# One decoder block in fp32: a fixed engine order between mixer output and feed-forward, 128-column modulation products, and the root's bias in the last norm

## The chip, the cores and the metric

The kernel runs on one core of a Trainium2 chip. The metric is the device time of one execution in microseconds (us), as the median of several runs. Before the change it is 968.55 us (three runs, 968.13 to 969.51).

## The reference, cut to what matters

A decoder block over 512 tokens of width 1024: two parallel mixers (retention, short gated convolution), a sigmoid-gated merge, an output projection, and a SwiGLU feed-forward of width 2816. Both norms are modulated by vectors computed from a conditioning vector `c`. All data are float32.

```python
mod = silu(c) @ ada_w + ada_b
sh_m, sc_m, gt_m, sh_f, sc_f, gt_f = split(mod, 6)

h = rmsnorm(x, norm_mix_g) * (1 + sc_m) + sh_m
q, k, v, g_ret, b_cv, c_cv, u_cv, g_a, g_b = split(h @ w_in, ...)
y_a = (silu(g_ret) * y_ret) @ ret_w_out        # y_ret: retention of q, k, v
y_b = (b_cv * conv(c_cv * u_cv)) @ conv_w_out
merged = sigmoid(g_a) * y_a + sigmoid(g_b) * y_b
x = x + gt_m * (merged @ mix_w_out)

h = rmsnorm(x, norm_ffn_g) * (1 + sc_f) + sh_f
f = (silu(h @ ffn_w_gate) * (h @ ffn_w_up)) @ ffn_w_down
x = x + gt_f * f
return rmsnorm(x, final_norm_g)
```

## The kernel before, in words

**Products.** Every float32 operand is split into a high and a low part (`hi` is a cast on ScalarE, `lo` the difference on VectorE), and each product is three fast matmuls, low by high, high by low and high by high (`mm3`). Activations stand by feature, 128 features by 512 tokens, in `Hh`/`Hl` (input of the mixers) and `Gh`/`Gl` (input of the feed-forward). Weights come through three `raw` buffers of 1 MB each; a load waits until the split of an earlier weight has read its buffer. Four PSUM banks (`acc`) hold accumulators, two (`aux`) the transposes.

**Start.** In the first 20 us `x` is normalised and transposed. The modulation vectors of the first 256 features come from `ada_w`: TensorE takes three of the eight row blocks as products of `ada_m` with one column of `cs` (`mod_row`), VectorE sums the other five into `acc_m`, and `mod_sums` brings those sums to features by a product with one column of ones. These are plain float32 matmuls, so the trace shows two records for each. Products that nobody reads (`busy`, tile `idle`) stand between them. Then `mod_scale` and `mod_shift` make `a_m` and `s_m` on VectorE, ScalarE makes `Hh` from them, and the first projections (`p_c`, `p_u`, `p_b`, `p_k`) begin. The same happens for the feature blocks 2, 4 and 6, between halves of a block's 21 projection products. In this stage the order on each engine is written out: while an engine's `strict` flag is set, the wrapper `InTurn` (L62) ties each instruction behind the one before.

**Between mixers and feed-forward.** `tm_gemm` makes the output projection by token block: for each half `h` of the 1024 columns four groups `mix` of 128 tokens by 512, each of 24 matmuls. For `h == 1` `add_gated` forms the new `x1`, `half_ss` its sum of squares on ScalarE, and `norm2` the root, its reciprocal and the scaled rows `xn`; one group later eight transposes `tx`, the modulated `h`, `Gh` (ScalarE) and `Gl` (VectorE) follow. `first_ffn` computes the first 256 gate and up columns in two halves of 256 tokens (four accumulators by two halves by 24 matmuls), so that its first half needs token blocks 0 and 1 alone. The low parts of its up weights (`w_fu_l`) are made on GpSimd. No order is fixed here: a scheduler places the instructions.

**End.** The down projection's last part goes by token block. For each, `row_rstd` adds the two partial sums of squares on VectorE, takes the root on ScalarE with `eps_t` as its bias, and the reciprocal on VectorE; the two halves of the output leave by two transfers on SP's queue. The last token block is cut in two parts of 256 columns.

Of the kernel before, what the change touches and what calls it, by code (L numbers as in the profile page):

```python
# [70 lines left out]
def block_kernel(ctx, tc, x, c, positions, ada_w, ada_b, norm_mix_g, w_in, conv_w, ret_w_out,  # L71
# [179 lines left out]
    def row_rstd(s, name):  # L251
        r = sp.tile([P, 1], F32, tag="rr", name=name + "_r")
        vec.tensor_tensor(r, s[:, 0:1], s[:, 1:2], ALU.add)
        act.activation(r, r, AF.Sqrt, scale=1.0 / D, bias=eps_t)
        vec.reciprocal(r, r)
        return r

# [624 lines left out]
    def norm2(t):  # L882
        r = row_rstd(ss2[t], f"n2_{t}")
        xn = []
        for h in range(2):
            xn.append(scr(f"xn2_{t}{h}"))
            vec.tensor_scalar_mul(xn[h], x1[t][h], r)

        def rest():
            ts = slice(t * P, (t + 1) * P)  # L890
            for h in range(2):
                tx = aux(f"tx2_{t}{h}", [P, 4, P])
                for k in range(4):
                    nc.tensor.transpose(tx[:, k, :], xn[h][:, k * P:(k + 1) * P], ident)
                ks = slice(4 * h, 4 * h + 4)
                h32 = scr(f"h232_{t}{h}", F32, [P, 4, P])
                for k in range(4):
                    q = slice(4 * h + k, 4 * h + k + 1)
                    if k % 2:
                        act.activation(h32[:, k, :], tx[:, k, :], AF.Identity,  # L900
                                       scale=mod["a_f"][:, q], bias=mod["s_f"][:, q])
                    else:
                        vec.tensor_scalar(h32[:, k, :], tx[:, k, :], mod["a_f"][:, q],
                                          mod["s_f"][:, q], ALU.mult, ALU.add)
                act.copy(Gh[:, ks, ts], h32)
                vec.tensor_tensor(Gl[:, ks, ts], h32, Gh[:, ks, ts].bitcast(F32), ALU.subtract)

        after(1, rest)
# [13 lines left out]
    for h in range(2):  # L922
        groups = [acc(f"mix{h}_{t}") for t in range(NT)]
        for t in tm_gemm(mix_w_out[0], merged, 0, KT, h, groups, 4 if h == 0 else 0, "mix"):
            tick()
            add_gated(t, h, groups[t], "gt_m")
            half_ss(x1[t][h], ss2[t], h, f"n2_{t}")
            if h == 1:
                norm2(t)


    def first_ffn():

        ws, pts = list(early_w), [acc(f"p_fg0{i}") for i in range(2)]
        raw = load_raw(ffn_w_up[0], 0, KT, 0, 2 * P, "w_fu0")
        for i in range(2):
            ws.append(split(raw[:, :, i * P:(i + 1) * P], [P, KT, P], f"w_fu0{i}", pool))
            pts.append(acc(f"p_fu0{i}"))
        for half in range(2):
            for i in range(4):  # L940
                fm_gemm(pts[i], ws[i][0], ws[i][1], Gh, Gl, slice(half * HS, half * HS + HS))
                if half == 0 and i == 0:
                    tick()
                if half == 1 and i >= 2:
                    yield i - 2, pts[i - 2], pts[i]
# [96 lines left out]
```

## Time and profile before

| what | value |
|---|---|
| median of three runs | 968.55 us |
| time of the profiled execution | 968.18 us |
| its span, first to last instruction | 966.4 us |
| TensorE busy | 953.5 us, 99% of the span |
| VectorE, ScalarE, GpSimd busy | 556.9, 340.9, 14.9 us |
| mean granted TensorE clock | 0.995 |
| DMA | 120.98 MB, mean 125 GB/s |

The span leaves out 1.8 us of the execution's time. TensorE counts as busy while a matmul is in its pipeline, so 99% does not mean that matmuls follow each other as closely as they can. The granted clock is a share of 2.4 GHz: 0.5 is the lower level, 1.2 GHz.

### The profile page before, as it was taken

How to read it: one execution, taken by the hardware profiler on the slowest of the kernel's cores; microseconds unless marked ns; L12 is line 12 of the kernel's file. 1: busy time of each engine (PE TensorE's matmuls, PEld its weight loads, DVE VectorE, ACT ScalarE, POOL GpSimd, SP SyncE). 2: the span in 40 equal slices, each digit the busy share in tenths (PEclk: the TensorE clock that was granted, in tenths of full speed). 3: DMA queues.
4: the chain of work that ended last, by engine and by line, in shares of the span. 5: the costliest groups of instructions: out<-in, count | busy, mean ns of one | idle time of the engine just before them, and what ended most of it. 6: DMA issues, size and time to landing. Idle time of an engine off the chain costs nothing.

```text
span 966.4 us, 11389 instructions
## 1 busy us (share of the span) xinstructions
PE 953.5 (99%) x4647; PEld 807.1 (84%) x4647; DVE 556.9 (58%) x841; ACT 340.9 (35%) x505; POOL 14.9 (2%) x22
## 2 busy tenths in 40 slices
PE   8999999999999999999999998999999999999997
PEld 8898889888888888888888887988888888888886
DVE  5888875959674855654574458346533433333354
ACT  7534434444443423222223336423322122222223
POOL 2001000000000000000000002000000000000000
PEclk9999999999999999999999999999999999999999
DMA  9943233141222247774553542234433223331302
GB/s 307 335 150 119 89 98 98 55 142 55 87 87 88 86 122 189 213 190 138 174 178 125 175 131 63 91 126 150 161 98 121 87 87 89 119 120 66 110 1 87
DMA packets 109044, 120.98 MB, mean 125 GB/s; under 512 B 3700, under 2 KB 96928, under 8 KB 108992
## 3 DMA queue, kind: packets, MB, share of 16 engines
q1 hardware_dynamic: 108768, 120.08, 39.6%
q8 instruction: 36, 0.59, 0.3%
q0 software_dynamic: 224, 0.18, 0.1%
q14 instruction: 16, 0.13, 0.0%
HBM read 118.15 MB, written 2.10 MB: 124 GB/s over the span
## 4 chain that ended last, share of the span: by engine, by line
PE 94%; DVE 2%; DMA 1%; ACT 1%; issue 0%; SPq 0%; ACTq 0%; DVEq 0%
PE p_fu L64 12%; PE p_fg L64 12%; PE dn L64 12%; PE p_v L64 5%; PE p_ga L64 5%; PE p_gb L64 5%; PE p_yb L64 5%; PE p_ya L64 5%; PE mix L64 4%; PE p_q L64 4%; PE p_k L64 4%; PE p_g L64 3%; PE p_u L64 3%; PE p_b L64 3%; PE p_c L64 3%; PE y L64 2%
## 5 line engine op out<-in xcount | busy, mean ns | idle before, releaser
L64 PE MATMUL p_fu<-Gl,w_fu_h 128*128 128x512 f32 (+1 forms) x192 | 71.4, 372 | 0.0
L64 PE MATMUL p_fu<-Gh,w_fu_l 128*128 128x512 f32 (+1 forms) x192 | 71.3, 371 | 0.0
L64 PE MATMUL p_fu<-Gh,w_fu_h 128*128 128x512 f32 (+1 forms) x192 | 71.3, 371 | 0.0
L64 PE MATMUL dn<-w_dn_h,fa_l 128*128 128x512 f32 (+1 forms) x176 | 67.5, 384 | 0.0
L64 PE MATMUL dn<-w_dn_l,fa_h 128*128 128x512 f32 (+1 forms) x176 | 67.5, 383 | 0.0
L64 PE MATMUL dn<-w_dn_h,fa_h 128*128 128x512 f32 (+1 forms) x176 | 67.4, 383 | 0.0
L64 PE MATMUL p_fg<-Gh,w_fg_l 128*128 128x512 f32 x160 | 62.3, 389 | 0.0
L64 PE MATMUL p_fg<-Gl,w_fg_h 128*128 128x512 f32 x160 | 62.3, 389 | 0.0
L64 PE MATMUL p_fg<-Gh,w_fg_h 128*128 128x512 f32 x160 | 62.3, 389 | 0.0
L64 DVE TENSOR_TENSOR w_dn_l<-w_dn,w_dn_h 128x1024 fp32r<-128x1024 f32 x22 | 26.9, 1224 | 57.5 <-ACT w_dn_h L64 57.5
L64 DVE TENSOR_TENSOR w_fg_l<-w_fg,w_fg_h 128x1024 fp32r<-128x1024 f32 x20 | 24.5, 1224 | 56.0 <-ACT w_fg_h L64 56.0
L64 ACT CAST w_fu_h<-w_fu 128x1024 fp32r<-128x1024 f32 x22 | 23.2, 1053 | 71.3 <-PE p_fu L64 38.4
L64 ACT CAST w_dn_h<-w_dn 128x1024 fp32r<-128x1024 f32 x22 | 23.1, 1050 | 65.6 <-PE dn L64 39.5
L64 DVE TENSOR_TENSOR fg<-p_fu,fg 128x512 f32<-128x512 f32 x22 | 15.2, 690 | 49.2 <-PE p_fu L64 49.2
L64 PEld LDWEIGHTS p_fu<-Gh,w_fu_h 128*128 128x128 f32 x192 | 36.2, 188 | 6.2
L64 PEld LDWEIGHTS p_fu<-Gl,w_fu_h 128*128 128x128 f32 x192 | 36.2, 188 | 6.2
L64 PEld LDWEIGHTS p_fu<-Gh,w_fu_l 128*128 128x128 f32 x192 | 36.2, 188 | 6.2
L64 ACT ACTIVATE fg<-p_fg 128x512 f32<-128x512 f32 x22 | 13.2, 598 | 79.6 <-PE p_fg L64 79.6
L64 PEld LDWEIGHTS dn<-w_dn_h,fa_l 128*128 128x128 f32 x176 | 33.1, 188 | 6.7
L64 PEld LDWEIGHTS dn<-w_dn_l,fa_h 128*128 128x128 f32 x176 | 33.1, 188 | 6.5
L64 PEld LDWEIGHTS dn<-w_dn_h,fa_h 128*128 128x128 f32 x176 | 33.1, 188 | 6.4
L64 PE MATMUL p_v<-w_v_h,Hh 128*128 128x256 f32 x128 | 36.2, 283 | 0.0
(343 smaller groups left out, 2522.0 us busy)
## 6 DMA issues: line engine op xcount, KB each, us to landing
w_fg<-in_ffn_w_gate_dram SPq DMA_DIRECT2D x11, 1024.0 KB, 5.4
w_fu<-in_ffn_w_up_dram SPq DMA_DIRECT2D x11, 1024.0 KB, 5.5
w_dn<-in_ffn_w_down_dram SPq DMA_DIRECT2D x10, 1024.0 KB, 5.0
ada_m<-in_ada_w_dram SPq DMA_DIRECT2D x32, 256.0 KB, 6.1
ada_f<-in_ada_w_dram SPq DMA_DIRECT2D x32, 256.0 KB, 4.3
...
```

Source lines behind the costliest of these rows:

```text
L64: self.last = op(*args, **kw)
```

## The change

It has four parts.

1. **Modulation products.** `mod_row` and `mod_sums` stream 128 equal columns (a broadcast of `cs`, all of `ones32`) where they streamed one, and the vectors are read from every 128th column. At the start all four products of row block 7 stand ahead of the sums, and two `busy` products follow instead of four.
2. **Mixer output to feed-forward.** For `h == 1` the order on TensorE, VectorE and ScalarE is written out. The transposes of a token block stand three matmuls before the end of the next group. VectorE's second `Gl` and ScalarE's second `Gh` of a block go behind the scaled rows of the next one.
3. **No GpSimd there.** The low parts of the first up weights are made on VectorE (`up_lo`), one ahead of token block 2's modulation, one ahead of token block 3's. In `first_ffn` the second up column block runs once over 512 tokens instead of twice over 256.
4. **Last norm.** The sum over the first half of the columns is scaled and increased by `EPS` as soon as it is there, and the root takes it as its bias, so that the addition on VectorE ahead of the root goes. The very last transfer is issued from ScalarE's queue.

The core of the diff:

```diff
         for i in cols:
-            mm(banks[i % 2][:, i:i + 1], lhsT=ada_raw["m", j][k][:, i * P:(i + 1) * P],
-               rhs=cs[:, k:k + 1], start=first and (i == 0 or i == 1 and banks is apart), stop=False)
+            mm(banks[i % 2][:, i * P:(i + 1) * P], lhsT=ada_raw["m", j][k][:, i * P:(i + 1) * P],
+               rhs=cs[:, k:k + 1].to_broadcast([P, P]),
+               start=first and (i == 0 or i == 1 and banks is apart), stop=False)
...
-            mm(banks[i % 2][:, i:i + 1], lhsT=a[:, i * P:(i + 1) * P], rhs=ones32[:, 0:1],
+            mm(banks[i % 2][:, i * P:(i + 1) * P], lhsT=a[:, i * P:(i + 1) * P], rhs=ones32,
...
-    mod_row(0, 7, apart, False, (0, 1, 2))
+    mod_row(0, 7, apart, False)
     mod_sums(a, apart, False, (0, 2))
-    mod_row(0, 7, apart, False, (3,))
     mod_sums(a, apart, False, (1, 3))
-    busy(4)
+    busy(2)
...
+    def mixed(t, k):
+        if t == 3 and k == 3:
+            up_hi(0)
+            up_lo(0)
+        if t and k == 6:
+            norm2_transposed(t - 1)
+            norm2_mod(t - 1, 0, vec)
+            for h in range(2):
+                norm2_mod(t - 1, h, act)
+            norm2_hi(t - 1, 0)
+
+    groups = [acc(f"mix1_{t}") for t in range(NT)]
+    for t in tm_gemm(mix_w_out[0], merged, 0, KT, 1, groups, 0, "mix", between=mixed):
+        pe.strict = vec.strict = act.strict = True
+        add_gated(t, 1, groups[t], "gt_m")
+        half_ss(x1[t][1], ss2[t], 1, f"n2_{t}")
+        if t:
+            norm2_mod(t - 1, 1, vec)
+        norm2_scaled(t)
+        if t:
+            norm2_hi(t - 1, 1)
+            norm2_lo(t - 1, 1)
...
+        part(0, 0, KT, halves[0])
+        part(1, 0, 5, halves[0])
+        up_hi(1)
+        up_lo(1)
+        norm2_transposed(3)
+        for h in range(2):
+            norm2_mod(3, h, vec)
+            norm2_mod(3, h, act)
+            norm2_hi(3, h)
+            norm2_lo(3, h)
+        pe.strict = vec.strict = act.strict = False
+        part(1, 5, KT, halves[0])
+        part(2, 0, KT, halves[0])
+        part(0, 0, KT, halves[1])
+        part(2, 0, KT, halves[1])
+        yield 0, pts[0], pts[2]
+        part(1, 0, KT, halves[1])
+        part(3, 0, KT, slice(0, S))
+        yield 1, pts[1], pts[3]
...
+                        vec.tensor_scalar(ss3[t][:, 0:1], ss3[t][:, 0:1], 1.0 / D, EPS, ALU.mult,
+                                          ALU.add)
...
-                r = row_rstd(ss3[t][:, cs.start // HS:], f"nf_{t}")
+                r = sp.tile([P, 1], F32, tag="rr", name=f"nf_{t}_r")
+                i = 1 + cs.start // HS
+                act.activation(r, ss3[t][:, i:i + 1], AF.Sqrt, scale=1.0 / D, bias=ss3[t][:, 0:1])
+                vec.reciprocal(r, r)
...
-                    nc.sync.dma_start(o2[t, i], o)
+                    (nc.sync if i or t < NT - 1 else nc.scalar).dma_start(o2[t, i], o)
```

The instructions move at three places. The first is TensorE's queue ahead of the first projection. `mods` and `p_k_126` are the two banks that take the modulation products, `acc_m_262` is VectorE's sum. Before:

```order
L62 MATMUL idle<-ident 128x128 x5
L62 MATMUL mods<-cs,ada_m_4_141 128x1
L62 MATMUL p_k_126<-cs,ada_m_4_141 128x1
L62 MATMUL mods<-cs,ada_m_4_141 128x1
L62 MATMUL mods<-ones_84,acc_m_262 128x1 x2
L62 MATMUL p_k_126<-cs,ada_m_4_141 128x1
L62 MATMUL p_k_126<-ones_84,acc_m_262 128x1 x2
L62 MATMUL idle<-ident 128x128 x4
L62 MATMUL p_c_290<-Hh,w_c_0_h 128x512
```

And now:

```order
L62 MATMUL idle<-ident 128x128 x5
L62 MATMUL mods<-cs,ada_m_4_141 128x128
L62 MATMUL p_k_126<-cs,ada_m_4_141 128x128
L62 MATMUL mods<-cs,ada_m_4_141 128x128
L62 MATMUL p_k_126<-cs,ada_m_4_141 128x128
L62 MATMUL mods<-ones_84,acc_m_262 128x128 x2
L62 MATMUL p_k_126<-ones_84,acc_m_262 128x128 x2
L62 MATMUL idle<-ident 128x128 x2
L62 MATMUL p_c_288<-Hh,w_c_0_h 128x512
```

The fourth product of row block 7 moved ahead of the sums, all have 128 columns, and two idle products are gone.

The second place is VectorE's queue from token block 1's modulation to token block 2's scaled rows. `h_1x` and `h_2x` are the modulated blocks, `n_2_r` is token block 2's root, `xn_2x` its scaled rows. Before:

```order
L64 TENSOR_SCALAR h_10_4875<-tx_10_4870,a_f,s_f 128x128
L64 TENSOR_SCALAR h_11_4887<-tx_11_4882,a_f,s_f 128x128
L64 TENSOR_TENSOR x_2_1_4549<-x_2_1_4549,dx_gt_m_0_4894 128x512
L64 TENSOR_TENSOR Gl<-h_10_4875,Gh 128x4x128
L64 TENSOR_TENSOR Gl<-h_11_4887,Gh 128x4x128
L64 TENSOR_TENSOR n_2_r<-n2s_4564 128x1
L64 RECIPROCAL n_2_r<-n_2_r 128x1
L64 TENSOR_SCALAR xn_20_4903<-x_2_0_4548,n_2_r 128x512
L64 TENSOR_SCALAR xn_21_4905<-x_2_1_4549,n_2_r 128x512
L64 TENSOR_TENSOR w_fg_l<-w_fg_5216,w_fg_h 128x1024
L64 TENSOR_SCALAR h_20_4936<-tx_20_4931,a_f,s_f 128x128
```

And now:

```order
L62 TENSOR_TENSOR x_2_1_4547<-x_2_1_4547,dx_gt_m_0_4887 128x512
L62 TENSOR_SCALAR h_11_4880<-tx_11_4870,a_f,s_f 128x128 x2
L62 TENSOR_TENSOR n_2_r<-n2s_4562 128x1
L62 TENSOR_TENSOR Gl<-h_10_4875,Gh 128x4x128
L62 RECIPROCAL n_2_r<-n_2_r 128x1
L62 TENSOR_SCALAR xn_20_4899<-x_2_0_4546,n_2_r 128x512
L62 TENSOR_SCALAR xn_21_4901<-x_2_1_4547,n_2_r 128x512
L62 TENSOR_TENSOR Gl<-h_11_4880,Gh 128x4x128
L62 TENSOR_TENSOR w_fu_lo<-w_fu_4917,w_fu_hi 128x1024
L62 TENSOR_SCALAR h_20_4942<-tx_20_4932,a_f,s_f 128x128 x2
```

One `Gl` now stands between the root's sum and its reciprocal, the other behind the scaled rows, and the first up weight's low part ahead of the next modulation.

The third place is the same queue at token block 3, the last one. Before:

```order
L64 TENSOR_SCALAR xn_30_4964<-x_3_0_4550,n_3_r 128x512
L64 TENSOR_SCALAR xn_31_4966<-x_3_1_4551,n_3_r 128x512
L64 TENSOR_SCALAR h_30_5015<-tx_30_5010,a_f,s_f 128x128
L64 TENSOR_SCALAR h_31_5027<-tx_31_5022,a_f,s_f 128x128
L64 TENSOR_SCALAR h_30_5015<-tx_30_5010,a_f,s_f 128x128
L64 TENSOR_SCALAR h_31_5027<-tx_31_5022,a_f,s_f 128x128
L64 TENSOR_TENSOR Gl<-h_30_5015,Gh 128x4x128
L64 TENSOR_TENSOR Gl<-h_31_5027,Gh 128x4x128
L64 TENSOR_TENSOR fg_0_5178<-p_fu_4980,fg_0_5178 128x512
```

And now:

```order
L62 TENSOR_SCALAR xn_30_4966<-x_3_0_4548,n_3_r 128x512
L62 TENSOR_SCALAR xn_31_4968<-x_3_1_4549,n_3_r 128x512
L62 TENSOR_TENSOR Gl<-h_21_4947,Gh 128x4x128
L62 TENSOR_TENSOR w_fu_lo<-w_fu_4917,w_fu_hi 128x1024
L62 TENSOR_SCALAR h_30_5033<-tx_30_5023,a_f,s_f 128x128 x2
L64 TENSOR_TENSOR w_fg_l<-w_fg_5190,w_fg_h 128x1024 x2
L62 TENSOR_TENSOR Gl<-h_30_5033,Gh 128x4x128
L62 TENSOR_SCALAR h_31_5040<-tx_31_5028,a_f,s_f 128x128 x2
L62 TENSOR_TENSOR Gl<-h_31_5040,Gh 128x4x128
L64 TENSOR_TENSOR fg_0_5128<-p_fu_4978,fg_0_5128 128x512
```

Three subtractions of whole weight blocks (`w_fu_lo`, `w_fg_l` twice) now stand between token block 3's scaled rows and its `Gl`.

## Rows read from the trace of the kernel before

**Rows 1.** The page: busy shares, and the chain that ended last by engine.
```profile
PE 953.5 (99%) x4647; PEld 807.1 (84%) x4647; DVE 556.9 (58%) x841; ACT 340.9 (35%) x505; POOL 14.9 (2%) x22
...
PE 94%; DVE 2%; DMA 1%; ACT 1%; issue 0%; SPq 0%; ACTq 0%; DVEq 0%
```
**Rows 2.** Stretches: us, busy us of each engine (instructions), PEclk, DMA share, GB/s.
```profile
18.00:20.00 2.00, 2.00 (x12) 2.00 (x12) 1.35 (x6) 1.67 (x3) 0.00 (x0) 0.54 1.11 342
20.00:22.00 2.00, 2.00 (x9) 1.72 (x9) 1.76 (x4) 1.97 (x5) 0.00 (x0) 0.61 1.09 346
...
595.60:597.60 2.00, 1.99 (x10) 1.99 (x11) 1.80 (x3) 1.28 (x3) 0.00 (x0) 0.50 0.85 257
```
**Rows 3.** Timeline of PE, start: start us, us, what, [idle before <-releaser].
```profile
2.10 5.11 PE L62 MATMUL idle<-ident 128*128 128x128 f32 x34
...
14.79 1.36 PE L62 MATMUL idle<-ident 128*128 128x128 f32 x10
...
17.12 0.78 PE L62 MATMUL mods<-ones,acc_m 128*128 128x1 f32 x4 [0.30 <-DVE acc_m L62]
...
18.70 2.06 PE L62 MATMUL idle<-ident 128*128 128x128 f32 x8
20.41 1.20 PE L62 MATMUL p_c<-Hh,w_c_h 128*128 128x512 f32 x2
...
24.25 0.62 PE L62 MATMUL p_c<-Hl,w_c_h 128*128 128x512 f32 x2
```
**Rows 4.** Timeline of VectorE and ScalarE, start.
```profile
17.94 0.22 DVE L62 SCALAR_TENSOR_TENSOR a_m<-mods,vecs,b_m 128x1 f32<-128x1 f32 x1 [0.48 <-PE mods L62]
...
18.33 0.81 ACT L62 ACTIVATE Hh<-xT,s_m,a_m 128x512 fp32r<-128x512 f32 x1 [0.54 <-DVE s_m L62]
...
21.55 0.69 DVE L62 TENSOR_TENSOR Hl<-xT,Hh 128x512 fp32r<-128x512 f32 x1
```
**Rows 5.** Timeline of PE at feature block 4.
```profile
40.38 0.95 PE L62 MATMUL mods<-ones,acc_m 128*128 128x1 f32 x8
41.19 0.71 PE L62 MATMUL p_c<-Hl,w_c_h 128*128 128x512 f32 x2
```
**Rows 6.** Timeline of GpSimd, 540 to 620 us.
```profile
588.71 2.41 POOL L64 TENSOR_TENSOR w_fu_l<-w_fu,w_fu_h 128x1024 fp32r<-128x1024 f32 x1 [494.25 <-ACT w_fu_h L64]
592.00 2.48 POOL L64 TENSOR_TENSOR w_fu_l<-w_fu,w_fu_h 128x1024 fp32r<-128x1024 f32 x1 [0.89 <-ACT w_fu_h L64]
```
**Rows 7.** Timeline of VectorE, 565 to 612 us.
```profile
580.14 0.68 DVE L64 TENSOR_TENSOR dx_gt_m<-mix,gt_m 128x512 f32<-128x512 f32 x1
...
584.45 0.88 DVE L64 TENSOR_SCALAR xn<-x,n_r 128x512 f32<-128x512 f32 x2
...
589.87 2.40 DVE L64 TENSOR_TENSOR Gl<-h,Gh 128x512 fp32r<-128x512 f32 x2 [1.44 <-ACT Gh L64]
592.19 2.31 DVE L64 TENSOR_TENSOR n_r<-n2s 128x1 f32<-128x1 f32 x1
```
**Rows 8.** Timeline of PE, 555 to 625 us.
```profile
585.08 1.06 PE L894 MATMUL tx<-ident,xn 128*128 128x128 f32 x8
...
592.90 0.28 PE L64 MATMUL p_fg<-Gl,w_fg_0h 128*128 128x256 f32 x1
595.61 1.97 PE L894 MATMUL tx<-ident,xn 128*128 128x128 f32 x8 [2.43 <-DVE xn L64]
```
**Rows 9.** The chain that ended last: start us, us, what.
```profile
614.81 5.76 PE p_fu L64 x48
620.57 10.91 PE p_fg L64 x48
```
**Rows 10.** Timeline of VectorE, ScalarE and SP's queue, end.
```profile
961.46 0.16 DVE L64 TENSOR_TENSOR nf_r<-nfs 128x1 f32<-128x1 f32 x1 [0.18 <-ACT nf_j L64]
...
961.66 0.29 ACT L64 ACTIVATE nf_r<-nf_r,eps_t 128x1 f32<-128x1 f32 x1 [0.23 <-DVE nf_r L64]
...
963.12 0.38 SPq L1006 DMA_DIRECT2D out_dram<-o  x1
```

More of the change, by code (lines that the diff above doesn't have):

```diff
@@ L249, in half_ss @@
         act.activation(junk[:, 0:part.shape[-1]], part, AF.Square, accum_out=s[:, h:h + 1])
[L251 to L256, printed above, removed]
     ang, angh, ah = misc("ang"), misc("angh", F32R), misc("ah")
@@ L476, in block_kernel @@
     for k in range(2):
-        mod_scale("m", k, apart[k][:, 2 + k:3 + k])
-        mod_shift("m", k, apart[k][:, k:k + 1], 1)
+        mod_scale("m", k, apart[k][:, (2 + k) * P:(2 + k) * P + 1])
+        mod_shift("m", k, apart[k][:, k * P:k * P + 1], 1)
     w_hi("c", 0)
@@ L514, in block_kernel @@
         w_lo("c", j)
-        mod_cols("m", j, mods)
+        mod_cols("m", j, mods.rearrange("p (i n) -> p i n", n=P)[:, :, 0])
         for k in (j, j + 1):
@@ L833, in block_kernel, with tm_gemm @@
             gate_vec("gt_m")
-    def tm_gemm(src, acts, k0, nk, h, groups, early, name, cut=False):
+    def tm_gemm(src, acts, k0, nk, h, groups, early, name, cut=False, between=None):
         ws = []
@@ L864, in tm_gemm @@
                 one(k, i)
+                if between:
+                    between(part[0], k)
             yield part if cut else part[0]
@@ L880, in block_kernel @@
     ss2 = [sp.tile([P, 2], F32, tag="ss", name=f"n2s_{t}") for t in range(NT)]
-    def norm2(t):
-        r = row_rstd(ss2[t], f"n2_{t}")
-        xn = []
-        for h in range(2):
[L886 to L908, printed above, removed]
@@ new lines, in block_kernel, with norm2_scaled, norm2_transposed @@
+    xn2, h2, tx2 = {}, {}, {}
+    def norm2_scaled(t):
+        r = sp.tile([P, 1], F32, tag="rr", name=f"n2_{t}_r")
+        vec.tensor_tensor(r, ss2[t][:, 0:1], ss2[t][:, 1:2], ALU.add)
+        act.activation(r, r, AF.Sqrt, scale=1.0 / D, bias=eps_t)
+        if t:
+            norm2_lo(t - 1, 0)
+        vec.reciprocal(r, r)
+        for h in range(2):
+            xn2[t, h] = scr(f"xn2_{t}{h}")
+            vec.tensor_scalar_mul(xn2[t, h], x1[t][h], r)
+    def norm2_transposed(t):
+        for h in range(2):
+            tx2[t, h] = aux(f"tx2_{t}{h}", [P, 4, P])
+            for k in range(4):
+                transpose(tx2[t, h][:, k, :], xn2[t, h][:, k * P:(k + 1) * P], ident)
@@ new lines, in norm2_mod @@
+    def norm2_mod(t, h, eng):
+        if (t, h) not in h2:
+            h2[t, h] = scr(f"h232_{t}{h}", F32, [P, 4, P])
+        for k in range(4):
+            q = slice(4 * h + k, 4 * h + k + 1)
+            if k % 2 and eng is act:
+                act.activation(h2[t, h][:, k, :], tx2[t, h][:, k, :], AF.Identity,
+                               scale=mod["a_f"][:, q], bias=mod["s_f"][:, q])
+            elif not k % 2 and eng is vec:
+                vec.tensor_scalar(h2[t, h][:, k, :], tx2[t, h][:, k, :], mod["a_f"][:, q],
+                                  mod["s_f"][:, q], ALU.mult, ALU.add)
@@ L910, in block_kernel, with norm2_hi, norm2_lo @@
+    def norm2_hi(t, h):
+        act.copy(Gh[:, 4 * h:4 * h + 4, t * P:(t + 1) * P], h2[t, h])
+    def norm2_lo(t, h):
+        g = slice(4 * h, 4 * h + 4), slice(t * P, (t + 1) * P)
+        vec.tensor_tensor(Gl[:, g[0], g[1]], h2[t, h], Gh[:, g[0], g[1]].bitcast(F32),
+                          ALU.subtract)
     early_w = []
@@ L920, in block_kernel @@
         early_w.append((wh, wl))
[L922 to L929, printed above, removed]
-    def first_ffn():
[L934 to L945, printed above, removed]
+    groups = [acc(f"mix0_{t}") for t in range(NT)]
@@ new lines, in block_kernel, with up_hi, up_lo @@
+    for t in tm_gemm(mix_w_out[0], merged, 0, KT, 0, groups, 4, "mix"):
+        tick()
+        add_gated(t, 0, groups[t], "gt_m")
+        half_ss(x1[t][0], ss2[t], 0, f"n2_{t}")
+    wu = []
+    def up_hi(i):
+        if i == 0:
+            wu.append(load_raw(ffn_w_up[0], 0, KT, 0, 2 * P, "w_fu0"))
+        hi, lo = (wp.tile([P, KT, P], F32R, tag=z, name=f"w_fu0{i}_{z}") for z in ("hi", "lo"))
+        act.copy(hi, wu[0][:, :, i * P:(i + 1) * P])
+        wu.append((hi, lo))
+    def up_lo(i):
+        hi, lo = wu[1 + i]
+        vec.tensor_tensor(lo, wu[0][:, :, i * P:(i + 1) * P], hi.bitcast(F32), ALU.subtract)
@@ new lines, in first_ffn, with part @@
+    def first_ffn():
+        pts = [acc(f"p_f{m}0{i}") for m in "gu" for i in range(2)]
+        def part(i, k0, k1, ts):
+            for k in range(k0, k1):
+                wh, wl = (w[k] if isinstance(w, list) else w[:, k, :] for w in (early_w + wu[1:])[i])
+                mm3(pts[i][:, ts], wh, wl, Gh[:, k, ts], Gl[:, k, ts], k == 0, k == KT - 1)
+        halves = [slice(i * HS, (i + 1) * HS) for i in range(2)]
+        part(0, 0, KT, halves[0])
[3 more added lines that the diff above has]
+        norm2_transposed(3)
+        for h in range(2):
+            norm2_mod(3, h, vec)
[11 more added lines that the diff above has]
+        yield 1, pts[1], pts[3]
@@ L993, in block_kernel @@
                     xg[t] = scr(f"xg_{t}")
-                else:
-                    vec.tensor_tensor(ss3[t][:, 1:2], ss3[t][:, 0:1], ss3[t][:, 1:2], ALU.add)
+                if cs.stop < S:
+                    vec.scalar_tensor_tensor(ss3[t][:, 0:1], ss3[t][:, 1:2], 1.0 / D,
+                                             ss3[t][:, 0:1], ALU.mult, ALU.add)
                 vec.tensor_tensor(xg[t][:, cs], x1[t][h][:, cs], fg[h][:, cs], ALU.mult)
```

2 lines of the change are left out of this document (added).

## The prediction

> **What bounds the kernel now.** I read the page first: TensorE is busy for 99% of the span and makes 94% of the chain that ended last [rows 1]. So a change pays only where TensorE waits, runs at its lower clock, or has finished while others still work. The table of stretches then shows where the clock is low: the granted clock is 0.54 and 0.61 from 18 to 22 us and 0.50 from 595.6 to 597.6 us, which is the 1.2 GHz level [rows 2]; everywhere else it is close to 1.00. TensorE's timeline shows the waits around these two places, and the timeline's last microseconds the third place, where TensorE has ended. The change touches exactly these three, so I price each alone.
>
> **Start, part 1 of the change.** Before the clock falls, TensorE has run one-column products with two waits between them [rows 3]. The four idle products at 18.70 then take 1.71 us until the first `p_c` at 20.41; at the pace of the idle products at 14.79 (ten records to the next row, 0.12 us each) they would take 0.96. `Hh`, which `p_c` needs, was ready at 19.14 (18.33 plus 0.81) [rows 4]. So `p_c` starts 1.27 us later than its data allow. It then runs at half clock for another microsecond: its 15th matmul stands at 24.25, 3.84 us after the first, where 14 at 0.227 us (10.91/48 [rows 9]) are 3.18. In the changed order, two idle products fewer let TensorE be free at about 18.45, before `Hh`. The sums end a little sooner too, since their wait ended at 17.12 and at full clock two of them need 0.24 each and then their latency, so I put `a_m` 0.1 to 0.2 us earlier than 17.94 and `p_c` at about 19.05. If the clock stays at 2.4 GHz the 15th matmul then stands at 22.3: **1.95 us** earlier. Next in line behind it is `Hl`, ready at 22.24 before [rows 4] and some 0.15 us sooner now, which just fits.
>
> The clock is the assumption here. The nearest row for it is the start itself: idle products of 128 columns and transposes fill most of the time up to 14 us, and the granted clock stays at 1.00 until the one-column products prevail. I take it that the changed products look like the idle ones.
>
> Against this stands what 128 columns cost. On TensorE's path lie the four products and four sums of feature block 2 and the four sums each of blocks 4 and 6: 16 products, 32 records. One column takes 0.101 us a record (41.19 less 40.38, by 8 [rows 5]). For 128 columns the lowest row is the idle one at 14.79, 0.12 us a record; the highest is the first idle stretch, 5.11 us by 34, 0.15 us [rows 3]. By these two rows the cost is 0.6 to 1.6 us; a gain is excluded, since no product goes away. Eight transposes of 128 columns fit into 1.06 us with the last one's latency [rows 8], which suggests that even 0.12 is high, so I take **0.4 us** and keep 1.6 for the range.
>
> The Trainium skill (TensorE: Matmul & The Clock Gate, section Back-to-back issue gap) speaks against these columns: a warm matmul of up to 64 columns takes about 60 cycles, one of 128 takes 134. As an estimate from that page the 32 records cost 1.0 us more, and the sum below would be 5.7 instead of 6.3. The trace does not agree for this kernel, since a one-column record already takes 0.101 us [rows 5], four times those 60 cycles.
>
> Start: 1.95 less 0.4 is 1.55 us.
>
> **Mixers to feed-forward, parts 2 and 3.** TensorE stops between the `p_fg` matmul at 592.90 and the transposes at 595.61: 2.71 us, of which 0.12 is the matmul's own pace (5.76/48 [rows 9]). It waits for `xn` on VectorE [rows 8]. VectorE's rows say why: two `Gl` subtractions take 2.40 us together, where 0.69 is normal for one of this size [rows 4], and an addition of 128x1 takes 2.31, where 0.16 is normal [rows 10]. They end within a tenth or two of GpSimd's two subtractions (588.71 to 591.12, 592.00 to 594.48) [rows 6, 7]. So VectorE stands while GpSimd's instruction runs, once for over 1 us and once for 2.1. The transposes then take 1.97 us instead of 1.06 [rows 8], and the clock is low [rows 2] until about 598.3. From 595.6 to 598.3 TensorE does the work of 1.35 us, so 1.35 is lost. With GpSimd gone both losses go: 2.6 plus 1.35.
>
> What comes in its place? VectorE gets two subtractions of 128x1024, some 1.2 us each (a little under twice the 0.69 of one half as wide [rows 4]), at places where it must be on time. Before, the chain from a group's end to its scaled rows took 5.2 us (580.14 to 585.33) [rows 7]. In the new order TensorE has 21 matmuls until it needs them, 4.8 us. The new order takes one `Gl` (0.6 us of VectorE) and one `Gh` cast out of this chain and puts them behind it, and lets the other `Gl` run while ScalarE takes the root; that leaves 4.2 us by the same rows, half a microsecond of room. For token block 3 the room is 3 `mix` and 40 `p_fg` matmuls of 0.12 with no transposes between, 5.5 us, less 0.7 for the group's own last three; the chain is again some 4.2 plus 0.6 that VectorE is late because of `w_fu_lo`. This is about even. Last, the second half of `first_ffn` needs token block 3's `Gl`: VectorE reaches it after `w_fu_lo` and two `w_fg_l`, 3.6 us, from about 597, and ends it near 602.4; TensorE asks at about 602.35 (23 of 24 `p_fu` matmuls behind the transposes). Even again; I put no stall there, and up to one in the range.
>
> The second up column block runs 24 matmuls of 512 columns (0.227 us) instead of 48 of 256 (0.12): 5.76 less 5.45 is 0.3 us saved [rows 9]. The three matmuls that now follow the transposes move no work. The raw buffer of the first up weights is released about 4 us later than GpSimd released it, which delays a load that is used 30 us later: nothing.
>
> Transition: 2.6, 1.35 and 0.3 are **4.25 us**.
>
> **End, part 4.** From the addition `nf_r` at 961.46 to the root at 961.66 is 0.20 us [rows 10]. It goes once for token block 2, behind which VectorE's last stretch is queued without a gap, and once for token block 3: 0.4 us, less 0.05 for the longer fused sum. The last transfer is issued at 963.12 on SP's queue, right behind another; an issue takes 0.38 us there [rows 10]. On ScalarE's queue it need not wait for that one. No row shows an issue from ScalarE. Bounds are 0.4 us better (the other issue's time) and 0.2 worse (an issue half as long again). I take 0.15. The four small VectorE instructions for the bias stand where VectorE waits for matmuls. End: **0.5 us**.
>
> **Sum.** 1.55, 4.25 and 0.5 are 6.3 us off the profiled execution's 968.18: 961.9 us. The three runs' median is 0.4 above that execution; I don't add it, as two of the three runs and the profile lie within 0.4 us.
>
> **The rivals.**
>
> *The clock falls at the start all the same.* For it: two waits remain (for `acc_m` and for `Hh`), and the transposes and waits around them are the same. Against: the rows before 14 us. Then `p_c` starts at 19.05 at half clock and 2.35 us until 21.4 do half the work: 1.2 us less gain, 963.1 us.
>
> *Columns paid in full.* At 0.15 us a record, 1.6 us instead of 0.4: 963.1 us. The skill's figures above would make it 962.5.
>
> *A wait at token block 3.* The two `w_fg_l` and `w_fu_lo` stand ahead of `Gl` on VectorE. It decides as soon as VectorE is late at `h_30`; then TensorE waits up to the two `w_fg_l`, 2.3 us: 964.2 us.
>
> *GpSimd is not what holds VectorE.* If the stretched rows come from something else (a transfer, ScalarE), the wait stays: only 2.05 and 0.3 are gained, 965.9 us. Against it: both stretched rows end with GpSimd's.
>
> *Slower: the fixed order waits three times.* In the free order a late `xn` lets TensorE go on with other matmuls; now each of three transposes stands ahead of matmuls that don't need it. If the chain from a group's end to `xn` took 7.5 us instead of 4.2, each place would stop TensorE as long as the one before did, with the low clock behind it: three times 3.95 us, 11.85, on top of 961.9, which makes 973.7. It loses against before from about 2.1 us per place on. Against it: the longest such chain without GpSimd is 5.2 us.
>
> **How the numbers follow.** The forecast has 0.63, the clock 0.12, the columns 0.08, the wait at token block 3 0.10, GpSimd not guilty 0.05, the three waits 0.02. A measurement of this kernel tells about 0.2%, 1.9 us, from no change. Below 966.6 lie all but the last case, with some room for what I have not seen: faster 0.95, within 0.2% 0.03, slower 0.02. The range takes in the first four cases with a microsecond of small errors in the terms: 960.3 to 964.6.
>
> **What would show it.** Right: granted clock near 1.00 from 18 to 22 us and the first `p_c` near 19; no wait of TensorE over 0.5 us from 573 to 620 and a VectorE addition `n_r` of 0.16 us; a chain without `nf_r` on VectorE ahead of the root. Wrong: a clock near 0.5 in either place, `tx` rows that wait for `xn`, `p_fg` or `p_fu` rows that wait for `Gl`, or a last transfer that lands later after ScalarE's last instruction than before.

## The result and the profile after

The changed kernel takes **961.90 us** (median of four runs, 961.56 to 962.06) against 968.34 us for the kernel before (its three runs and a fourth of 966.57): a ratio of 0.9935 with a 95% interval of 0.9917 to 0.9952. Forecast were 961.9 us and a gain of over 0.2%; both came. The profiled execution took 962.06 us, its span is 960.3 us. One later execution of the kernel before took 1603.95 us at a granted clock of 0.555 and is left out of every number here.

The page's busy shares and chain, which answer to [rows 1]:

```profile
PE 949.9 (99%) x4619; PEld 802.7 (84%) x4619; DVE 555.9 (58%) x843; ACT 340.1 (35%) x505; POOL 10.1 (1%) x20
...
PE 96%; DVE 2%; ACT 1%; DMA 1%; issue 0%; SPq 0%; ACTq 0%
```

Busy TensorE time fell by 3.6 us with only 28 records fewer, so over half of the 6.1 us that went was time in which TensorE counted as busy. GpSimd lost two instructions of 2.4 us.

Stretches of the changed kernel (columns as in [rows 2]), the start and the passage to the feed-forward:

```profile
18.00:20.00 2.00, 1.60 (x12) 1.37 (x12) 1.17 (x5) 1.35 (x3) 0.00 (x0) 1.00 1.08 339
20.00:22.00 2.00, 2.00 (x11) 1.62 (x10) 1.76 (x4) 2.00 (x4) 0.00 (x0) 1.00 1.10 348
...
594.00:598.00 4.00, 4.00 (x36) 4.00 (x36) 3.91 (x9) 3.68 (x6) 0.00 (x0) 1.00 0.00 0
```

The granted clock is 1.00 where it was 0.54, 0.61 and 0.50. TensorE's timeline of the changed kernel, against [rows 3, 8]:

```profile
18.51 0.61 PE L62 MATMUL idle<-ident 128*128 128x128 f32 x4
19.51 0.73 PE L62 MATMUL p_c<-Hh,w_c_h 128*128 128x512 f32 x2 [0.40 <-ACT Hh L62]
...
22.82 0.62 PE L62 MATMUL p_c<-Hl,w_c_h 128*128 128x512 f32 x2
...
595.74 1.04 PE L62 MATMUL tx<-ident,xn 128*128 128x128 f32 x8
```

The first `p_c` now waits for its data (`Hh`), not for idle products, and the transposes of token block 3 wait for nothing. VectorE's timelines of the changed kernel, at the start against [rows 4] and in the passage against [rows 7]:

```profile
18.26 0.22 DVE L62 SCALAR_TENSOR_TENSOR a_m<-mods,vecs,b_m 128x1 f32<-128x1 f32 x1 [0.58 <-PE mods L62]
```

```profile
587.16 0.16 DVE L62 TENSOR_TENSOR n_r<-n2s 128x1 f32<-128x1 f32 x1 [0.31 <-ACT n_j L62]
587.24 0.68 DVE L62 TENSOR_TENSOR Gl<-h,Gh 128x512 fp32r<-128x512 f32 x1
...
588.03 0.88 DVE L62 TENSOR_SCALAR xn<-x,n_r 128x512 f32<-128x512 f32 x2
588.83 0.68 DVE L62 TENSOR_TENSOR Gl<-h,Gh 128x512 fp32r<-128x512 f32 x1
589.43 1.22 DVE L62 TENSOR_TENSOR w_fu_lo<-w_fu,w_fu_hi 128x1024 fp32r<-128x1024 f32 x1
...
598.11 2.35 DVE L64 TENSOR_TENSOR w_fg_l<-w_fg,w_fg_h 128x1024 fp32r<-128x1024 f32 x2
600.37 0.68 DVE L62 TENSOR_TENSOR Gl<-h,Gh 128x512 fp32r<-128x512 f32 x1
```

`n_r` takes 0.16 us instead of 2.31, each `Gl` 0.68, and the subtraction that came from GpSimd 1.22. The end, from the timeline of all engines, against [rows 10]:

```profile
955.30 0.18 ACT L64 ACTIVATION_READ_ACCUMULATOR nf_j<-x 128x1 f32 x1
955.52 0.29 ACT L64 ACTIVATE nf_r<-nfs 128x1 f32<-128x1 f32 x1
...
956.79 0.38 ACTq L1072 DMA_DIRECT2D out_dram<-o  x1
```

The root follows its sum on ScalarE directly.

To see where the time went I cut every execution at four rows: the beginning of the last four `acc_m` sums on VectorE (a time that the transfers set), the first `p_c` matmul that reads `Hl` (the 15th matmul from the first `p_c` on), the first `dx_gt_m` of the `h == 1` groups, and the first `dx_gt_f` of token block 2 in the last part. The table holds all profiled executions of this study; its last five columns are the times between these rows, in us. The printed spans are rounded to 0.1 us; the last column takes them from the packed traces to 0.01 (966.41 before, 960.27 after). The fourth column tells how long TensorE was busy in the 2 us from 16 to 18, where it may have to wait for `acc_m`.

| execution | columns | clock 18 to 22 us | TensorE busy 16 to 18 us | to `acc_m` | `acc_m` to `p_c` | to `dx_gt_m` | to `dx_gt_f` | to the end |
|---|---|---|---|---|---|---|---|---|
| before | 1 | 0.54, 0.61 | 1.68 | 15.01 | 9.24 | 549.24 | 381.81 | 11.11 |
| after | 128 | 1.00, 1.00 | 2.00 | 15.22 | 7.60 | 549.18 | 377.67 | 10.60 |
| e1_columns | 128 | 1.00, 1.00 | 1.80 | 14.95 | 7.60 | 549.19 | 380.49 | 11.10 |
| e2_idle | 1 | 0.94, 0.50 | 1.78 | 15.52 | 9.08 | 549.11 | 382.01 | 11.10 |
| e3_low_on_dve | 1 | 0.60, 0.55 | 1.54 | 14.99 | 9.20 | 549.11 | 378.32 | 11.10 |
| e4_bias | 1 | 1.00, 1.00 | 1.53 | 15.20 | 7.62 | 549.11 | 381.96 | 10.60 |
| e5_low_on_pool | 128 | 1.00, 1.00 | 2.00 | 14.90 | 7.61 | 549.29 | 378.65 | 10.60 |
| e6_memset | 128 | 1.00, 1.00 | 2.00 | 14.78 | 7.91 | 549.28 | 378.19 | 10.59 |
| e7_v_on_dve | 128 | 1.00, 1.00 | 1.96 | 15.37 | 7.98 | 548.07 | 377.66 | 10.60 |
| e8_queue | 128 | 1.00, 1.00 | 2.00 | 15.01 | 7.61 | 549.37 | 377.66 | 10.59 |
| e9_v_timed | 128 | 1.00, 1.00 | 2.00 | 15.26 | 7.62 | 547.90 | 377.66 | 10.60 |
| e10_after_again | 128 | 1.00, 1.00 | 2.00 | 15.18 | 7.59 | 549.19 | 377.66 | 10.59 |
| e11_before_again | 1 | 1.00, 1.00 | 2.00 | 14.64 | 7.63 | 549.32 | 382.06 | 11.10 |

From before to after the columns lose 1.64 at the start, 4.14 in the passage and 0.51 at the end, and 0.06 in between; 0.21 comes back because the first transfers landed later in that execution. That is 6.14, as the spans have it; the two execution times differ by 6.12.

### The profile page after: what moved, and what is told of

Same layout as the page of the kernel before. It is cut to its first block, busy times and chain, and to the rows that moved or that the text cites. A ratio compares the mean times of both kernels' runs of the same rounds, so it can differ in the third digit from the quotient of the medians.

```text
span 960.3 us, 11325 instructions
## 1 busy us (share of the span) xinstructions
PE 949.9 (99%) x4619; PEld 802.7 (84%) x4619; DVE 555.9 (58%) x843; ACT 340.1 (35%) x505; POOL 10.1 (1%) x20
## 4 chain that ended last, share of the span: by engine, by line
PE 96%; DVE 2%; ACT 1%; DMA 1%; issue 0%; SPq 0%; ACTq 0%
PE p_fu L64 13%; PE p_fg L64 12%; PE dn L64 12%; PE p_v L64 5%; PE p_ga L64 5%; PE p_gb L64 5%; PE p_yb L64 5%; PE p_ya L64 5%; PE p_k L64 4%; PE p_q L64 4%; PE p_g L64 3%; PE p_u L64 3%; PE p_b L64 3%; PE p_c L64 3%; PE mix L64 3%; PE mix L62 2%
## 5 line engine op out<-in xcount | busy, mean ns | idle before, releaser
L64 PE MATMUL p_fu<-Gh,w_fu_l 128*128 128x512 f32 x160 | 62.3, 389 | 0.0
L64 PE MATMUL p_fu<-Gh,w_fu_h 128*128 128x512 f32 x160 | 62.3, 389 | 0.0
L64 PE MATMUL p_fu<-Gl,w_fu_h 128*128 128x512 f32 x160 | 62.2, 389 | 0.0
L64 ACT CAST w_fu_h<-w_fu 128x1024 fp32r<-128x1024 f32 x20 | 21.1, 1053 | 74.2 <-PE p_fu L64 41.8
L64 PE MATMUL p_v<-w_v_l,Hh 128*128 128x256 f32 x128 | 36.2, 283 | 0.0
L64 PE MATMUL p_v<-w_v_h,Hl 128*128 128x256 f32 x128 | 36.2, 283 | 0.0
L64 PEld LDWEIGHTS p_fg<-Gh,w_fg_h 128*128 128x128 f32 x160 | 30.0, 188 | 6.3
```

Source lines behind the costliest of these rows:

```text
L64: self.last = op(*args, **kw)
```

## The experiments

Single executions of the experiments are read by the table's columns. In the changed kernel, where nothing was touched, the passage and the end repeat to 0.01 us (377.66 and 377.67, 10.59 and 10.60) and the stretch in between to 0.2; at the start e6 and e7 lost 0.3 to 0.4 us more, because the weight block `w_u` landed late there. Theory: the clock makes the start's gain, GpSimd's conflict with VectorE that of the passage, and the root's bias with the transfer's queue that of the end.

**Start: the columns alone (e1_columns), and the idle products and order alone (e2_idle).** Both are made on the kernel before.

```diff
 # e1_columns, the same in mod_sums and where the vectors are read
-            mm(banks[i % 2][:, i:i + 1], lhsT=ada_raw["m", j][k][:, i * P:(i + 1) * P],
-               rhs=cs[:, k:k + 1], ...
+            mm(banks[i % 2][:, i * P:(i + 1) * P], lhsT=ada_raw["m", j][k][:, i * P:(i + 1) * P],
+               rhs=cs[:, k:k + 1].to_broadcast([P, P]), ...
 # e2_idle
-    mod_row(0, 7, apart, False, (0, 1, 2))
+    mod_row(0, 7, apart, False)
     mod_sums(a, apart, False, (0, 2))
-    mod_row(0, 7, apart, False, (3,))
     mod_sums(a, apart, False, (1, 3))
-    busy(4)
+    busy(2)
```

> The kernel before with the 128 equal columns alone (four idle products and the order of the sums as before). My theory, the columns keep the clock up: granted clock 0.95 to 1.00 from 18 to 22 us, the first p_c at 19.3 to 19.7, the 15th p_c matmul some 3.2 us behind it at 22.5 to 22.9. Rival, the waits for acc_m and Hh let it fall whatever the columns: 0.5 to 0.6 in that stretch, first p_c at 20.2 or later, the 15th at 24.0 or later. Rival, columns paid in full: from the 15th p_c matmul to the p_c row behind the sums of block 4 it takes 17.3 to 17.9 us, where before it is 16.94 (24.25 to 41.19); my term of 0.4 us expects 17.2.

> The kernel before with the new order of the sums and two idle products instead of four, but one column as before. My theory: the clock falls all the same (0.5 to 0.65 from 18 to 22 us), the first p_c comes 0.6 to 0.9 us earlier than 20.41 since the two products that are gone took 0.43 each, and its first microseconds run at half clock, so that the 15th stands at 23.4 to 23.7. Rival, the gain of the start is the idle products and the order, not the clock: clock near 1.00, 15th at 22.3 to 22.9.

TensorE's timeline with the columns alone; four idle products and the old order still stand ahead of `p_c`:

```profile
18.45 1.06 PE L62 MATMUL idle<-ident 128*128 128x128 f32 x8
19.26 0.71 PE L62 MATMUL p_c<-Hh,w_c_h 128*128 128x512 f32 x2
...
22.55 0.62 PE L62 MATMUL p_c<-Hl,w_c_h 128*128 128x512 f32 x2
...
38.69 1.05 PE L62 MATMUL mods<-ones,acc_m 128*128 128x128 f32 x8
39.49 0.71 PE L62 MATMUL p_c<-Hl,w_c_h 128*128 128x512 f32 x2
```

And with one column, two idle products and the new order, first TensorE's timeline, then the stretch:

```profile
19.70 1.18 PE L62 MATMUL p_c<-Hh,w_c_h 128*128 128x512 f32 x2 [0.29 <-ACT Hh L62]
...
24.60 0.62 PE L62 MATMUL p_c<-Hl,w_c_h 128*128 128x512 f32 x2
```

```profile
20.00:22.00 2.00, 2.00 (x6) 1.52 (x6) 1.57 (x3) 2.00 (x5) 0.00 (x0) 0.50 1.09 347
```

The execution with the columns alone has the whole 7.60 us of the change; the times were 965.1 and 968.62 us. Without the columns `p_c` starts sooner, but the clock is at its lower level afterwards instead of before, and the stage is as long as ever (9.08). I had expected 0.6 to 0.9 us from the idle products and got 0.16. The four sums of block 4 take 0.80 us to the next row with 128 columns (38.69 to 39.49) and 0.81 with one [rows 5], and from the `p_c` matmul at 22.55 to that next row it is 16.94 us in both: on TensorE the wide columns cost nothing that shows.

**Is the clock's fall certain? (e11_before_again, and e4_bias by its start).** Both have one column and the start of the kernel before, unchanged.

> The kernel before again, for its clock: with one column the start's clock fell in three of four profiled executions so far (9.1 to 9.2 us from acc_m's last sums to the 15th p_c matmul) and stayed up in one (7.62). My theory: it falls again (9.0 to 9.3 us), 967.8 to 969.0 us in all; by chance it may stay up, and then the time is 966.4 to 966.9 us and nothing else differs.

It stayed up: 966.55 us, with 7.63 in the start's column. A stretch of this second execution of the kernel before:

```profile
18.00:20.00 2.00, 2.00 (x15) 1.82 (x16) 1.57 (x4) 1.75 (x3) 0.00 (x0) 1.00 1.09 344
```

So with one column the clock fell in three of five profiled executions and stayed at 1.00 in two; with 128 columns it stayed up in all eight. Four of the five (all but e2) have the same instructions at the start, and there it fell in two of four. That one column lets the clock fall, as I had taken it, was too strong: with one column it was left to chance. The Trainium skill (TensorE: Matmul & The Clock Gate, section What's actually happening) says of a kernel's beginning that one and the same kernel has a different number of slow matmuls from run to run; these four executions vary likewise, and show it 18 us into the program.

The plain times agree. Of 14 timed executions of the kernel before, twelve took 967.97 to 969.51 us and two 966.39 and 966.57, about as much as e11; the nine of the changed kernel all lie between 961.56 and 962.06.

It is not shown that the columns are what keeps the clock up. TensorE's wait for `acc_m` changed as well. The stretch from 16 to 18 us of before, e4, e11, e1 and after, in this order:

```profile
16.00:18.00 2.00, 1.68 (x15) 1.48 (x13) 1.49 (x4) 0.62 (x1) 0.00 (x0) 1.00 1.10 342
16.00:18.00 2.00, 1.53 (x12) 1.28 (x11) 1.62 (x3) 0.62 (x1) 0.00 (x0) 1.00 1.11 341
16.00:18.00 2.00, 2.00 (x20) 1.91 (x18) 1.34 (x5) 0.66 (x2) 0.00 (x0) 1.00 1.10 339
16.00:18.00 2.00, 1.80 (x12) 1.35 (x11) 1.38 (x4) 0.62 (x1) 0.00 (x0) 1.00 1.11 340
16.00:18.00 2.00, 2.00 (x18) 1.90 (x17) 1.63 (x3) 0.62 (x1) 0.00 (x0) 1.00 1.11 345
```

In the seven executions with all of the change's start TensorE hardly waited there (1.96 to 2.00 us busy). With one column it waited in four (1.53 to 1.78), of which three lost the clock, and did not wait in e11, which kept it. With 128 columns it waited only in e1, which kept it, as e4 did with one column. So the change's start as a whole kept the clock up in seven of seven; that 128 columns alone do it, with the wait as it was, rests on one execution. Several more of e1 would tell.

**Passage: GpSimd away, order free (e3_low_on_dve).** On the kernel before.

```diff
-            ws.append(split(raw[:, :, i * P:(i + 1) * P], [P, KT, P], f"w_fu0{i}", pool))
+            ws.append(split(raw[:, :, i * P:(i + 1) * P], [P, KT, P], f"w_fu0{i}"))
```

> The kernel before with the low parts of the first up weights on VectorE, order free as before. My theory, GpSimd's subtractions are what stretches VectorE's rows: every Gl takes 0.7 us and n_r 0.16, no wait of TensorE over 0.5 us in 573 to 620 us, and from dx_gt_m of the first h==1 group to the first p_fg of the second half it is 43.1 to 43.6 us, where before it is 47.08 (573.49 to 620.57) and with the whole change 42.89. Rival, the written order is what pays: two subtractions of 1.2 us fall ahead of scaled rows, TensorE waits for xn for 1 us or more, 44.5 to 46.5 us. Rival, GpSimd is not guilty: rows stay at 2.3 to 2.4 us.

VectorE's timeline:

```profile
588.47 1.23 DVE L64 TENSOR_TENSOR w_fu_l<-w_fu,w_fu_h 128x1024 fp32r<-128x1024 f32 x1 [0.23 <-ACT w_fu_h L64]
589.68 1.29 DVE L64 TENSOR_TENSOR Gl<-h,Gh 128x512 fp32r<-128x512 f32 x2
590.89 0.15 DVE L64 TENSOR_TENSOR n_r<-n2s 128x1 f32<-128x1 f32 x1
591.76 1.23 DVE L64 TENSOR_TENSOR w_fu_l<-w_fu,w_fu_h 128x1024 fp32r<-128x1024 f32 x1 [0.72 <-ACT w_fu_h L64]
...
594.10 0.87 DVE L64 TENSOR_SCALAR xn<-x,n_r 128x512 f32<-128x512 f32 x2
```

All rows have their normal length. TensorE's order shifted, so the first `p_fg` of the second half is no longer the same mark; by the table the passage takes 378.32 us, 3.49 less than before (expected, from the marks, 3.5 to 4.0). The time was 964.49 us. Against the full change 0.65 us is left, of which the block of 512 columns should be 0.31 (5.76 less 5.45, my estimate of the prediction) and the rest I put down to the written order; neither was tried alone. Two subtractions did fall ahead of `xn`, as the rival had it, but TensorE's transposes waited only some 0.1 us for it.

**Passage: GpSimd back in the fixed order (e5_low_on_pool), and GpSimd only writing (e6_memset).** On the changed kernel; `vec` is VectorE, `pool` GpSimd.

```diff
 # e5_low_on_pool
-        vec.tensor_tensor(lo, wu[0][:, :, i * P:(i + 1) * P], hi.bitcast(F32), ALU.subtract)
+        pool.tensor_tensor(lo, wu[0][:, :, i * P:(i + 1) * P], hi.bitcast(F32), ALU.subtract)
 # e6_memset
-        vec.tensor_tensor(lo, wu[0][:, :, i * P:(i + 1) * P], hi.bitcast(F32), ALU.subtract)
+        with tc.issue_after(act.last.ins):
+            for _ in range(2):
+                pool.memset(lo.bitcast(F32), 0.0)
```

> The changed kernel with the low parts of the first up weights back on GpSimd, in the fixed order. My theory, a GpSimd subtraction stops VectorE wherever it runs: a VectorE instruction of two inputs (Gl, x or n_r) that meets it takes 1.5 to 2.4 us instead of 0.16 to 0.69, TensorE waits again for xn, Gl or w_fu_lo, and from dx_gt_m of the first h==1 group to the first p_fg of the second half it takes 43.5 to 47 us, where with the change it is 42.89. Rival, only the order was wrong before: VectorE is freed of 2.4 us, all rows keep their normal length, 42.6 to 42.9 us.

> As the run before it, but GpSimd writes zeros twice into the low part (some 1 us each) in place of the subtraction, so that it only writes; the low parts of the first up weights are left out of the computation. The Trainium skill (SBUF — State Buffer) has the conflict between a VectorE instruction with two inputs in SBUF and a GpSimd instruction that reads SBUF. By that rule: VectorE's rows keep 0.16 to 0.69 us and nothing waits, 42.5 to 42.9 us between the same marks. Rival, any GpSimd instruction holds VectorE while it runs: rows of 1 us and more beside the memsets.

GpSimd's timeline of the first of the two, then VectorE's:

```profile
588.98 2.57 POOL L64 TENSOR_TENSOR w_fu_lo<-w_fu,w_fu_hi 128x1024 fp32r<-128x1024 f32 x1 [496.22 <-ACT w_fu_hi L62]
595.32 2.58 POOL L64 TENSOR_TENSOR w_fu_lo<-w_fu,w_fu_hi 128x1024 fp32r<-128x1024 f32 x1 [3.77 <-ACT w_fu_hi L62]
```

```profile
589.81 0.73 DVE L62 TENSOR_SCALAR h<-tx,a_f,s_f 128x128 f32<-128x128 f32 x2 [0.50 <-PE tx L62]
590.94 0.69 DVE L62 TENSOR_TENSOR dx_gt_m<-mix,gt_m 128x512 f32<-128x512 f32 x1 [0.40 <-PE mix L62]
...
596.70 3.42 DVE L64 TENSOR_TENSOR w_fg_l<-w_fg,w_fg_h 128x1024 fp32r<-128x1024 f32 x2
```

The stall is back, but only once. GpSimd's first subtraction (588.98 to 591.55) meets `h` and `dx_gt_m`, which read their tensor from PSUM, and these keep 0.73 and 0.69 us. The second (595.32 to 597.90) meets `w_fg_l`, both of whose inputs lie in SBUF: 3.42 us for two instead of 2.35. VectorE, relieved of one subtraction of 1.2 us there, so comes to the next `Gl` at nearly the same time as with the change (600.04 against 600.37, in an execution that was 0.20 us ahead at the first `dx_gt_m`), while TensorE, whose free order behind token block 3 asks for it sooner, waits 0.27 us for `Gl` and then 0.37 for `Gh`. The passage takes 0.98 us longer than with the change and the kernel 962.81 us. So the price of GpSimd here is set by which VectorE instruction it happens to meet.

The memsets started earlier than intended, all four in a row, as soon as their buffers were free. GpSimd's timeline, then VectorE's, then TensorE's:

```profile
585.94 4.04 POOL L64 MEMSET w_fu_lo<- 128x1024 f32 x4 [492.90 <-PE mix L62]
```

```profile
587.21 0.68 DVE L62 TENSOR_TENSOR Gl<-h,Gh 128x512 fp32r<-128x512 f32 x1
...
588.00 2.26 DVE L62 TENSOR_SCALAR xn<-x,n_r 128x512 f32<-128x512 f32 x2
```

```profile
590.41 0.63 PE L62 MATMUL tx<-ident,xn 128*128 128x128 f32 x4 [0.47 <-DVE xn L62]
```

`Gl` with two inputs runs beside the memsets in its normal time, as that page of the Trainium skill has it. `xn` does not: 2.26 us for two instead of 0.88. TensorE waited 0.47 us for the second of them and the passage took 0.52 us more than with the change; I had expected nothing. The same page of the Trainium skill (SBUF — State Buffer, section Who interferes with whom) says that a scaling can run in a mode which takes the shared ports and then contends with GpSimd. I had quoted the one rule and overlooked the other; here both agree with the rows.

**End: bias alone (e4_bias, on the kernel before), transfer back on SP's queue (e8_queue, on the changed kernel).** The first takes over the change's lines in the last norm word for word, all but the one that the second undoes:

```diff
 # e8_queue
-                    (nc.sync if i or t < NT - 1 else nc.scalar).dma_start(o2[t, i], o)
+                    nc.sync.dma_start(o2[t, i], o)
```

> The kernel before with the root's bias alone (last transfer still from SP's queue). From dx_gt_f of token block 2 in the last part (955.30) to the span's end (966.4) it is 11.1 us before and 10.6 with the whole change. My theory: 10.7 to 10.8, 0.35 from the two additions that are gone. Rival, the scaled sum takes the addition's place on VectorE and nothing is gained: 11.0 to 11.1; the transfer's queue then makes all of the end's 0.47.

> The changed kernel with the very last transfer back on SP's queue. From dx_gt_f of token block 2 in the last part to the span's end the change has 10.63 us. My theory: 10.75 to 10.85, the issue waits for the other one's on SP. Rival, no difference (10.6 to 10.7), if an issue from ScalarE costs what it saves.

SP's queue with the last transfer back on it:

```profile
956.95 0.38 SPq L1072 DMA_DIRECT2D out_dram<-o  x1
```

The end takes 10.60 us with the bias alone, against 11.10 to 11.11 in all five executions without it. It takes 10.59 with the last transfer on SP, where the changed kernel has 10.60 and 10.59. (The 10.63 in the expectation came from the rounded span.) The bias makes all of the gain, more than the 0.35 that I expected of it; ScalarE's queue makes none, though the last issue stands 7.12 us behind `dx_gt_f` there and 7.30 on SP's queue. (e4's 966.26 us is mostly its start, where the clock stayed up.)

**A better kernel (e7_v_on_dve, e9_v_timed beside e10_after_again).** The traces of both kernels hold one more GpSimd subtraction that holds up VectorE. GpSimd's, VectorE's and TensorE's timelines of the changed kernel:

```profile
90.67 2.40 POOL L64 TENSOR_TENSOR w_v_l<-w_v,w_v_h 128x1024 fp32r<-128x1024 f32 x1 [2.95 <-ACT w_v_h L64]
```

```profile
91.83 1.78 DVE L64 TENSOR_TENSOR k_a<-k_a,k_b 128x512 f32<-128x512 f32 x1
```

```profile
101.78 0.50 PE L64 MATMUL st<-q_l,k_h 128*128 128x512 f32 x1 [0.73 <-DVE q_l L64]
```

`k_a` is held until GpSimd's instruction ends at 93.07 and then takes some 0.5 us; TensorE later waits for `q_l`, which stands behind it on VectorE.

```diff
-        for i, pt in value_proj(p, pool if p == 1 else None):
+        for i, pt in value_proj(p):
```

> The changed kernel with the last GpSimd subtractions, of w_v for the second pair of heads (85.28 and 90.67 us), on VectorE. My theory: one falls into VectorE's idle time before ropeC (3.6 us), the other behind q_l; k_a<-k_a,k_b takes 0.69 instead of 1.78, the two gaps of TensorE at 94.5 and 100.7 us (0.36 and 0.89) go: 1.0 to 1.3 us less, 960.6 to 961.0. Rival, VectorE's 2.3 us more fall on the path to q_l or sm, and TensorE waits as long: within 0.4 us of 961.9, or slower.

> The same kernel as the run with w_v's low parts on VectorE, timed in five rounds on one chip with the changed kernel. My theory, the two gaps of TensorE at 94.5 and 100.7 us are gone for good: 1.0 to 1.3 us below the changed kernel's median, 960.6 to 961.0. Rival, the single look's 961.45 was all there is: 0.2 to 0.6 us below.

> The changed kernel again, for the comparison: 961.6 to 962.2 us; in its start the granted clock stays at 1.00 and the 15th p_c matmul stands 7.6 us behind the beginning of acc_m's last four sums, as in every run with 128 columns so far. If the clock's fall is chance with any column count, one more sample may show 9.0 to 9.3 us.

The first execution took 961.45 us, more than expected, with the gain in its column (548.07) and 0.38 us lost at the start, where a weight block (`w_u`) landed late. Timed, it has **960.47 us** (five runs, 960.26 to 960.83) against 961.92 for the changed kernel timed beside it (five runs, 961.61 to 962.00) and 968.25 for the kernel before: 0.9923 (0.9910 to 0.9936) of the kernel before, where the changed kernel has 0.9936 (0.9922 to 0.9950). The medians differ by 1.45 us, where 1.0 to 1.3 was expected; by the column it is 547.90 against 549.19, 1.29 us. The changed kernel itself came out as expected, with 7.59 at the start. VectorE's timeline of the better kernel (e9):

```profile
85.24 1.23 DVE L64 TENSOR_TENSOR w_v_l<-w_v,w_v_h 128x1024 fp32r<-128x1024 f32 x1 [0.17 <-ACT w_v_h L64]
...
92.22 0.68 DVE L64 TENSOR_TENSOR k_a<-k_a,k_b 128x512 f32<-128x512 f32 x1
...
102.35 1.22 DVE L64 TENSOR_TENSOR w_v_l<-w_v,w_v_h 128x1024 fp32r<-128x1024 f32 x1
```

The two subtractions stand where VectorE had time, and `k_a` is short again.

## Why the prediction was right

**Start, 1.55 forecast, 1.64 measured.** The two terms behind it were both off. "If the clock stays at 2.4 GHz ... 1.95 us earlier" was sized too high by 0.3: the stage went from 9.24 to 7.60. Its parts were put wrongly, too. I put `a_m` "0.1 to 0.2 us earlier"; behind the beginning of VectorE's four sums it comes 0.11 us later (18.26 less 15.22 is 3.04, before 17.94 less 15.01 is 2.93), and so it does in every execution with 128 columns. I also let two idle products fewer bring part of it; with the clock up the first `p_c` stands 4.32 us behind the same row with four of them (e1, e4, e11) and 4.29 with two. The clock is all of the gain, and the idle products are merely slow when it is low. "I take 0.4 us" for the columns was too much: the eight records of block 4 show nothing, and what `a_m` loses disappears behind the idle products. The two errors cancelled, which is luck. The Trainium skill's 60 against 134 cycles, an estimate of 1.0 us, does not show in these products; the row of 0.101 us for one column spoke right.

What the prediction left out is that the fall is chance. It took the profiled execution as the kernel's own; with the clock up, the kernel before takes some 1.6 us less (966.55 us). The median stands where the profiled execution does, and that was enough here. Its assumption that 128 columns "look like the idle ones" to the clock came true in eight executions, but was shown without the shorter wait in one alone.

**Passage, 4.25 forecast, 4.14 measured.** The mechanism is shown: e3 takes GpSimd's work away alone and regains 3.49, e5 puts it back and the stall returns. The term of 1.35 for the low clock can be read from e1, whose passage has the same instructions and the same wait for `xn`, but there the clock stayed up. TensorE's timeline and the stretch behind it:

```profile
593.84 1.09 PE L894 MATMUL tx<-ident,xn 128*128 128x128 f32 x8 [2.43 <-DVE xn L64]
```

```profile
595.50:597.50 2.00, 2.00 (x19) 2.00 (x18) 2.00 (x6) 1.41 (x4) 0.00 (x0) 1.00 0.88 306
```

It took 380.49 us against 381.81 to 382.06 in the four executions where the clock fell: 1.3 to 1.6 us. The wait itself stood in all five (2.42 to 2.44 us behind the end of the last matmul's row; the forecast's 2.6 counts from 0.12 us behind its beginning). From e1 to the change the passage loses another 2.82 us, close to the forecast's 2.6 for the wait and 0.3 for the block of 512 columns. One reading was loose: of the stretched rows only `n_r` ends with GpSimd's instruction (594.50 and 594.48); the pair of `Gl` ends at 592.27, 1.15 us behind GpSimd's first, and an undisturbed pair takes 1.29 (e3). "About even", twice, for token block 3 was right: in the change `Gl` ends at 601.05 and TensorE's first matmul that reads it stands at 601.11, so the room was next to nothing, and e5, where `w_fg_l` was stretched by 1.07 us just there, waited and lost 0.98.

**End, 0.5 forecast, 0.51 measured.** The split was wrong. "0.20 us ... once for token block 2 and once for token block 3 ... less 0.05" was too small: the two steps shrank by 0.25 and 0.26 (from `dx_gt_f` of block 2 to that of block 3, 3.39 to 3.14; from there to the last root, 2.97 to 2.71), and the longer sum cost nothing. The 0.15 for ScalarE's queue was nothing; here too the errors cancelled.

**The rivals.** Columns in full, the three waits and an innocent GpSimd are excluded by e1, the profile after and e3. The wait at token block 3 did not come, with 0.06 us of room. The clock's fall at the start is excluded only as far as eight profiled executions and nine timed ones of the changed kernel go.
